# Turning the attention probabilities by a product with a diagonal matrix of inverse sums, in a two-layer hybrid backbone

## The chip, the cores and the metric

One core of a Trainium2 chip runs the whole kernel. The metric is the device time of one execution in microseconds (us), less is better. The core's engines go by short names: PE multiplies matrices (PEld is its loading of the stationary operand), DVE is the vector engine, ACT the scalar engine that also does the exponentials, POOL the general engine, and SP issues most of the transfers.

## What is computed

A backbone of two layers works on 512 latent tokens and 256 context tokens of width 1024, all in 32-bit floats. Each layer has a modulated RMSNorm, one input projection whose columns feed three head groups, an output projection with a gated residual, and a SwiGLU. The three groups are a latent attention (MLA, 4 heads; a latent token reads all 768 tokens, a context token the 256 of the context), a two-dimensional neighbourhood attention (NA, 4 heads; a block of 128 queries reads 256 local keys and the 256 context keys), and a gated delta rule in two directions. In the second layer context tokens aren't needed behind the attentions, so that only the 512 latent tokens are queries there. Both attentions end in the same way:

```python
def softmax_attention(q, k, v, scale):
    s = jnp.einsum('bqhd,bkhd->bhqk', q, k).astype(jnp.float32) * scale
    p = jax.nn.softmax(s, axis=-1).astype(v.dtype)
    return jnp.einsum('bhqk,bkhd->bqhd', p, v)
```

## The kernel before

Everything is unrolled; a tile framework orders the instructions of each engine in one list at build time, with a simulated timeline, and sets the semaphores. Large products are made of three products of reduced 32-bit parts (helper `mm3`; high and low halves), smaller ones of one product of plain 32-bit operands (helper `mm`, line 104, the line under which all products appear in the trace). A layer goes through these stages: input projection (tiles `acc_in`) with convolutions and the preparation of the delta rule; the neighbourhood attention (function `attention`, from line 850); the latent attention (from line 1183); the output projection (`acc_o`, `acc_o2`); the SwiGLU (`acc_gu`, `acc_d`).

The neighbourhood attention loops over 2 pairs of heads and, in each, over blocks of 128 queries (4 of latent tokens, and in the first layer 2 of context tokens). The latent attention loops in the same way. At each block the function `beside` may put other work into the order: one or two steps of the delta rule (`scan` and `inverse`, with the products `ks`, `yp`, `sp`, `qs`, `oa` on the full array and `pp`, `yq` on parts of it), by the hand-written counts in `DNS`; in the first layer's neighbourhood attention also two columns of modulation weights per block (`acc_ada`). So both attentions share PE and DVE with the delta rule. The first layer's latent attention also has the first part of the output projection (`acc_o`) beside it.

For one block and one head of a pair (`j`) the steps are these; lines of the neighbourhood attention first, of the latent attention second:

1. PE makes the scores in PSUM (`s_na`; `s_mla`).
2. DVE finds the row maximum (lines 870 to 876; 1199 and 1202), ACT writes the exponentials to the tile `pr` in SBUF and their sums to a small tile (877 and 878; 1206).
3. DVE adds the sums and takes the inverse (882 and 883; 1210 and 1212).
4. DVE multiplies `pr` by the inverse, one number per row, in place (884; 1213). A tile has 512 columns in the neighbourhood attention, 768 in the latent one, and 256 for context queries in both.
5. PE turns each block of 128x128 of `pr` with `PE.transpose` against the identity into PSUM (`tp_na`, 889; `tp_mla`, 1217): 4, 6, or 2 blocks for context queries.
6. ACT or DVE copies the result to SBUF (`pt`, 891; 1218), and behind both heads PE multiplies it with the values (`o_na`; `o_mla`).

`pr` has two buffers; the PSUM tiles of step 5 and of the last products share three.

Of the kernel before, what the change touches and what calls it, by code (L numbers as in the profile page):

```python
# [9 lines left out]
F32 = mybir.dt.float32  # L10
F32R = mybir.dt.float32r
AF = mybir.ActivationFunctionType
ALU = mybir.AluOpType
# [4 lines left out]
P = 128  # L18
D = 1024
KD = D // P  # L20
TL, TC = 512, 256
T = TL + TC
# [80 lines left out]
def mm(nc, out, lhsT, rhs, start=True, stop=True):  # L103
    nc.tensor.matmul(out, lhsT, rhs, start=start, stop=stop)  # L104
# [258 lines left out]
def layer(tc, nc, a, l, es_x, xT, env, nx):  # L363
    e = env
    V, S, G, PE = nc.vector, nc.scalar, nc.gpsimd, nc.tensor
    tt, stt, pool, C, ident, wtiles, gemm, dump, dram = e.tt, e.stt, e.pool, e.C, e.ident, e.wtiles, e.gemm, e.dump, e.dram
# [11 lines left out]
    def eb(name):  # L378
        tag = EB_TAG.get(name, "e")
        return psE.tile([P, 512], F32, tag=tag, name=name, bufs=EB[tag])  # L380
# [142 lines left out]
    tp = eb("ab_tp")  # L523
# [30 lines left out]
    tp = eb("gc")  # L554
# [286 lines left out]
    sn = None  # L841
# [5 lines left out]
    def attention():  # L847
        for pair in range(2):
            gm = gms[pair]
            o_na = sn.tile([P, T], F32, tag="o_na", name="o_na", bufs=1)  # L850
            grid = lambda t: t[:, LAT].rearrange("p (r c) -> p r c", c=GW)
            qh, ql, kh, kl = nqh[:, pair], nql[:, pair], nkh[:, pair], nkl[:, pair]
            for qt in range(nT // P):
                is_ctx = qt >= 4
                tok = slice(qt * P, (qt + 1) * P)
                c0 = (0, 8, 24, 32, 0, 0)[qt]
                var = (0, 1, 1, 2, 0, 0)[qt]
                vb = ((0, 1), (6, 7), (7, 8), (2, 3), (), ())[qt] + (4, 5)
                lo_ = 256 if is_ctx else 0
                pts = []  # L860
                for j in range(2):
                    hs = slice(64 * j, 64 * j + 64)
                    cutk = lambda t: grid(t)[hs, :, c0:c0 + 32].rearrange("p r (b c) -> p b r c", b=2)
                    s_ = att_bank("s_na")
                    if not is_ctx:
                        mm3(nc, s_[:, 0:256], (qh[hs, tok], ql[hs, tok]), (cutk(kh), cutk(kl)))
                    mm3(nc, s_[:, 256:512], (qh[hs, tok], ql[hs, tok]), (kh[hs, CTX], kl[hs, CTX]))
                    st_ = sn.tile([P, 8], F32, tag="st", name="st", bufs=4)
                    pr = sn.tile([P, 512], F32, tag="pr", name="pr", bufs=2)
                    V.reduce_max(out=st_[:, 0:1], in_=s_[:, 256:512], axis=AX.X)  # L870
                    if is_ctx:
                        V.tensor_scalar(out=st_[:, 2:3], in0=st_[:, 0:1], scalar1=-1.0, scalar2=None, op0=ALU.mult)
                    else:
                        V.tensor_tensor_reduce(out=pr[:, 0:256], in0=s_[:, 0:256], in1=gm[:, j, var].rearrange("p b r c -> p (b r c)"),
                                               scale=1.0, scalar=NEG, op0=ALU.add, op1=ALU.max, accum_out=st_[:, 1:2])
                        V.tensor_scalar(out=st_[:, 2:3], in0=st_[:, 0:1], scalar1=st_[:, 1:2], scalar2=-1.0, op0=ALU.max, op1=ALU.mult)
                        S.activation(out=pr[:, 0:256], in_=pr[:, 0:256], func=AF.Exp, bias=st_[:, 2:3], accum_out=st_[:, 3:4])
                    S.activation(out=pr[:, 256:512], in_=s_[:, 256:512], func=AF.Exp, bias=st_[:, 2:3], accum_out=st_[:, 4:5])
                    if is_ctx:
                        V.reciprocal(out=st_[:, 5:6], in_=st_[:, 4:5])  # L880
                    else:
                        tt(out=st_[:, 6:7], in0=st_[:, 3:4], in1=st_[:, 4:5], op=ALU.add)
                        V.reciprocal(out=st_[:, 5:6], in_=st_[:, 6:7])
                    V.tensor_scalar(out=pr[:, lo_:512], in0=pr[:, lo_:512], scalar1=st_[:, 5:6], scalar2=None, op0=ALU.mult)
                    tp = att_bank("tp_na")
                    nb = 2 if is_ctx else 4
                    for b in range(nb):
                        o2 = lo_ + b * P
                        PE.transpose(tp[:, b * P:(b + 1) * P], pr[:, o2:o2 + P], ident)  # L889
                    pt = sn.tile([P, 512], F32, tag="pt", name="pt", bufs=3)  # L890
                    (S.copy if j == 0 else V.tensor_copy)(out=pt[:, 0:nb * P], in_=tp[:, 0:nb * P])
                    pts.append(pt)
                o_ = att_bank("o_na")
                for b in range(len(vb)):
                    for j in range(2):
                        hd = 2 * pair + j
                        mm(nc, o_[j * 64:j * 64 + 64, 0:P], nav[:, vb[b], hd * 64:hd * 64 + 64], pts[j][:, b * P:(b + 1) * P],
                           b == 0, b == len(vb) - 1)
                if is_ctx:
                    S.copy(out=o_na[:, tok], in_=o_[:, 0:P])  # L900
                else:
                    S.copy(out=grid(o_na)[:, :, 16 * qt:16 * qt + 16], in_=o_[:, 0:P].rearrange("p (r c) -> p r c", c=16))
                if qt == nT // P - 1:
                    nc.sync.dma_start(out=d_o[2 + pair][:, 0:nT], in_=o_na[:, 0:nT])
                    if l == 0 and e.dbg is not None and "na" in e.dbg:
                        nc.sync.dma_start(out=e.dbg["na"][:, pair], in_=o_na)
                yield True
# [214 lines left out]
    sa = pool(es_w, f"sb_mla{l}", side=B_)  # L1122
# [31 lines left out]
    for pair in range(2):  # L1154
# [27 lines left out]
        for qt in range(nT // P):  # L1182
            beside(ada, sa)
            is_ctx = qt >= 4
            kst = ((CTX, 4, 2),) if is_ctx else ((LAT, 0, 4), (CTX, 4, 2))
            kcols = slice(TL, T) if is_ctx else slice(0, T)
            tok = slice(qt * P, (qt + 1) * P)
            pts = []
            for j in range(2):
                kh, kl, qh, ql = qk[j]  # L1190
                s8 = sa.tile([P, 8], F32, tag="st", name="st", bufs=4)
                pr = sa.tile([P, T], F32, tag="pr", name="pr", bufs=2)
# [17 lines left out]
                    tt(out=s8[:, 5:6], in0=den, in1=s8[:, 4:5], op=ALU.add)  # L1210
                    den = s8[:, 5:6]
                V.reciprocal(out=s8[:, 6:7], in_=den)
                V.tensor_scalar(out=pr[:, kcols], in0=pr[:, kcols], scalar1=s8[:, 6:7], scalar2=None, op0=ALU.mult)
                for i, (st_, b0, nb) in enumerate(kst):
                    tp = att_bank("tp_mla")
                    for b in range(nb):
                        PE.transpose(tp[:, b * P:(b + 1) * P], pr[:, (b0 + b) * P:(b0 + b + 1) * P], ident)
                    (V.tensor_copy if (b0 == 0) == (j == 0) else S.copy)(out=pt[:, st_], in_=tp[:, 0:nb * P])
                pts.append(pt)
            o_ = att_bank("o_mla")  # L1220
            b0 = kst[0][1]
# [245 lines left out]
```

## Time and profile before

| | |
|---|---|
| Median of 3 runs | 2146.63 us (2128.88, 2146.63, 2149.4) |
| The profiled execution | 2147.42 us, its span 2145.6 us |
| Mean granted clock of PE | 0.961 of full speed |
| Busy: PE, DVE, POOL, ACT | 2008.8, 1176.9, 758.7, 714.1 us |

The profile is of one execution on the chip. Times count from the start of the span. A busy PE isn't PE at its peak, since products are pipelined and their ends are modelled. The granted clock is the share of full speed that PE's throttle gave; 0.50 is the lower of its two levels.

### The profile page before, as it was taken

What the parts mean: (1) busy time and instruction counts of PE and PEld (TensorE: products, weight loads), DVE (VectorE), ACT (ScalarE), POOL (GpSimd) and SP (SyncE); (2) the same over time, 40 slices, a digit from 0 to 9 for tenths busy, and PEclk for the clock granted to TensorE, in tenths of its full rate; (3) what the DMA queues carried; (4) which work ended last, traced back from release to release, by engine and by line L of the source; (5) the groups of instructions that cost most, each with busy time, mean ns of one, the idle gap of its engine ahead of it and who ended that gap; (6) DMA issues with size and microseconds to landing.
All of it is one profiled execution on the core that took longest, in us unless ns stands there. A gap on an engine that the chain in (4) does not pass through costs nothing. (4 is left out here: it accounts for less than half of the span.)

```text
span 2145.6 us, 32031 instructions
## 1 busy us (share of the span) xinstructions
PE 2008.8 (94%) x12770; PEld 1699.3 (79%) x12770; DVE 1176.9 (55%) x2045; ACT 714.1 (33%) x1385; POOL 758.7 (35%) x540
## 2 busy tenths in 40 slices
PE   6899998998998999999999998889899889999998
PEld 4788787887787888888888876777688678888887
DVE  4888814768656447347343458882559654222123
ACT  5333323335444121121122344324334443222233
POOL 3465233113323222232323445623202252444444
PEclk9999998999999999999999999999679999999999
DMA  7324253542322435244342512424222232332332
GB/s 278 80 79 147 80 157 100 176 155 77 102 71 79 130 118 164 92 130 158 107 128 70 155 34 71 151 73 134 74 67 87 67 105 67 93 95 94 102 96 91
DMA packets 119309, 232.56 MB, mean 108 GB/s; under 512 B 30516, under 2 KB 55988, under 8 KB 119032
## 3 DMA queue, kind: packets, MB, share of 16 engines
q1 hardware_dynamic: 119160, 230.51, 34.2%
q8 instruction: 101, 1.65, 0.3%
q14 instruction: 48, 0.39, 0.1%
HBM read 199.46 MB, written 31.01 MB: 107 GB/s over the span
## 5 line engine op out<-in xcount | busy, mean ns | idle before, releaser
L217 POOL TENSOR_TENSOR wl<-wr,wh 128x1024 fp32r<-128x1024 f32 (+2 forms) x188 | 440.4, 2343 | 829.3 <-ACT wh L216 810.8
L216 ACT CAST wh<-wr 128x1024 fp32r<-128x1024 f32 (+2 forms) x190 | 193.5, 1019 | 717.9 <-PE acc_gu L104 289.2
L104 PE MATMUL acc_gu<-fh,wh 128*128 128x512 f32 (+1 forms) x1024 | 358.8, 353 | 9.6 <-ACT fh L304 8.7
L104 PE MATMUL acc_gu<-fl,wh 128*128 128x512 f32 (+1 forms) x1024 | 360.7, 353 | 4.1 <-DVE fl L305 4.1
L104 PE MATMUL acc_gu<-fh,wl 128*128 128x512 f32 (+1 forms) x1024 | 359.9, 352 | 0.0
L104 PE MATMUL acc_in<-hh,wh 128*128 128x512 f32 (+1 forms) x640 | 229.0, 362 | 16.9 <-ACT xp L491 6.2
L104 PE MATMUL acc_in<-hl,wh 128*128 128x512 f32 (+1 forms) x640 | 228.6, 358 | 3.0 <-DVE hl L305 2.0
L104 PE MATMUL acc_in<-hh,wl 128*128 128x512 f32 (+1 forms) x640 | 225.3, 356 | 2.1 <-POOL wl L217 2.0
L104 PEld LDWEIGHTS acc_gu<-fh,wh 128*128 128x128 f32 x1024 | 194.0, 190 | 37.2 <-ACT fh L304 11.0
L1348 DVE TENSOR_TENSOR av<-acc_gu,av 128x768 f32<-128x768 f32 (+1 forms) x44 | 36.3, 825 | 337.7 <-PE acc_gu L104 329.7
L104 PEld LDWEIGHTS acc_gu<-fl,wh 128*128 128x128 f32 x1024 | 195.0, 190 | 30.5 <-DVE fl L305 4.3
L104 PEld LDWEIGHTS acc_gu<-fh,wl 128*128 128x128 f32 x1024 | 194.8, 190 | 26.2
L104 PEld LDWEIGHTS acc_in<-hh,wh 128*128 128x128 f32 x640 | 125.1, 196 | 43.3 <-issue 8.1
L104 PE MATMUL acc_d<-al,wh 128*128 128x512 f32 (+1 forms) x444 | 157.2, 354 | 0.0
L104 PE MATMUL acc_d<-ah,wh 128*128 128x512 f32 (+1 forms) x444 | 157.2, 354 | 0.0
L104 PE MATMUL acc_d<-ah,wl 128*128 128x512 f32 (+1 forms) x444 | 156.1, 354 | 0.0
L254 DVE CUSTOM_DVE_ANT_0 junk<-wada,scb 128x1024 f32<-128x1024 f32 x112 | 144.1, 1286 | 7.9 <-DMA wada<-w_adaT 5.2
L104 PEld LDWEIGHTS acc_in<-hl,wh 128*128 128x128 f32 x640 | 125.7, 196 | 24.8 <-DVE hl L305 4.6
L104 PEld LDWEIGHTS acc_in<-hh,wl 128*128 128x128 f32 x640 | 124.8, 196 | 21.1 <-POOL wl L217 3.4
L1366 DVE SCALAR_TENSOR_TENSOR xT<-acc_d,mod,xT 128x512 f32<-128x512 f32 (+1 forms) x76 | 46.5, 634 | 155.4 <-PE acc_d L104 155.4
L501 DVE SCALAR_TENSOR_TENSOR cy<-xp,cw,cy 128x770 f32<-128x770 f32 (+1 forms) x96 | 118.9, 1239 | 22.5 <-ACT cy L499 20.4
L1352 DVE TENSOR_TENSOR al<-av,ah 128x768 fp32r<-128x768 f32 (+1 forms) x44 | 100.4, 2282 | 35.1 <-ACT ah L1351 35.1
(390 smaller groups left out, 3906.2 us busy)
## 6 DMA issues: line engine op xcount, KB each, us to landing
wr<-w_gu SPq DMA_DIRECT2D x88, 512.0 KB, 3.5
wada<-w_adaT SPq DMA_DIRECT2D x56, 512.0 KB, 3.3
wr<-w_in SPq DMA_DIRECT2D x48, 512.0 KB, 3.5
wr<-w_dn SPq DMA_DIRECT2D x32, 448.0 KB, 3.3
wada<-w_ada SPq DMA_DIRECT2D x24, 512.0 KB, 3.4
wada<-w_ada SPq DMA_DIRECT2D x8, 1024.0 KB, 8.3
wr<-w_dn SPq DMA_DIRECT2D x16, 512.0 KB, 3.5
xT<-xT SPq DMA_DIRECT2D x16, 384.0 KB, 5.3
```

The source lines that it names most:

```text
L104: nc.tensor.matmul(out, lhsT, rhs, start=start, stop=stop)
L216: S.copy(out=hi[:, sl], in_=raw[:, sl])
L217: eng.tensor_tensor(out=lo[:, sl], in0=raw[:, sl], in1=hi[:, sl].bitcast(F32), op=ALU.subtract)
L254: V.tensor_tensor_reduce(out=junk, in0=w, in1=scb[:, s], scale=1.0, scalar=0.0, op0=ALU.mult, op1=ALU.add, accum_out=mod[l][:, part, j, s: ...
L501: stt(out=y[:, :wid], in0=xp[:, j:j + wid], scalar=w_(j), in1=y[:, :wid], op0=ALU.mult, op1=ALU.add)
L1348: tt(out=av[:, :nT], in0=accs[1][:, :nT], in1=av[:, :nT], op=ALU.mult)
L1352: after.append(tt(out=l_[:, :nT], in0=av[:, :nT], in1=h_[:, :nT].bitcast(F32), op=ALU.subtract))
L1366: stt(out=xT[:, m, st_], in0=acc, scalar=mod[l][:, 5, m, s:s + 1], in1=xT[:, m, st_], op0=ALU.mult, op1=ALU.add)
```

## The change

Step 4 is taken away. Instead DVE multiplies the identity, a constant tile of 128x128, by the inverse of each row into a new tile `dg` (two buffers), a diagonal matrix. Step 5 becomes a product of each block of `pr` with `dg`: `mm(out, lhsT, rhs)` gives the transpose of `lhsT` times `rhs`, which is the turned block with each column multiplied by the inverse of its query. Copies and later products stay as they are.

```diff
@@ attention()
-                    V.tensor_scalar(out=pr[:, lo_:512], in0=pr[:, lo_:512], scalar1=st_[:, 5:6], scalar2=None, op0=ALU.mult)
+
+                    dg = sn.tile([P, P], F32, tag="dg", name="dg", bufs=2)
+                    V.tensor_scalar(out=dg, in0=ident, scalar1=st_[:, 5:6], scalar2=None, op0=ALU.mult)
                     tp = att_bank("tp_na")
                     nb = 2 if is_ctx else 4
                     for b in range(nb):
                         o2 = lo_ + b * P
-                        PE.transpose(tp[:, b * P:(b + 1) * P], pr[:, o2:o2 + P], ident)
+                        mm(nc, tp[:, b * P:(b + 1) * P], pr[:, o2:o2 + P], dg)
@@ latent attention
-            kcols = slice(TL, T) if is_ctx else slice(0, T)
...
                 V.reciprocal(out=s8[:, 6:7], in_=den)
-                V.tensor_scalar(out=pr[:, kcols], in0=pr[:, kcols], scalar1=s8[:, 6:7], scalar2=None, op0=ALU.mult)
+                dg = sa.tile([P, P], F32, tag="dg", name="dg", bufs=2)
+                V.tensor_scalar(out=dg, in0=ident, scalar1=s8[:, 6:7], scalar2=None, op0=ALU.mult)
                 for i, (st_, b0, nb) in enumerate(kst):
                     tp = att_bank("tp_mla")
                     for b in range(nb):
-                        PE.transpose(tp[:, b * P:(b + 1) * P], pr[:, (b0 + b) * P:(b0 + b + 1) * P], ident)
+                        mm(nc, tp[:, b * P:(b + 1) * P], pr[:, (b0 + b) * P:(b0 + b + 1) * P], dg)
```

## Rows read from the trace of the kernel before

**Rows 1.** The page, part 1: busy us, share of the span, instructions.
```profile
PE 2008.8 (94%) x12770; PEld 1699.3 (79%) x12770; DVE 1176.9 (55%) x2045; ACT 714.1 (33%) x1385; POOL 758.7 (35%) x540
```
**Rows 2.** Windows: stretch, its length, busy us by engine, PEclk, DMA share, GB/s.
```profile
362.00:482.00 120.00, 119.20 (x1483) 100.13 (x1482) 80.17 (x259) 40.71 (x137) 18.39 (x24) 1.00 0.51 162
515.00:560.00 45.00, 41.68 (x294) 32.19 (x293) 32.04 (x84) 22.72 (x77) 7.49 (x13) 0.91 0.31 103
580.00:642.00 62.00, 62.00 (x430) 52.92 (x429) 34.30 (x89) 24.95 (x59) 17.11 (x9) 1.00 0.20 62
1507.00:1520.00 13.00, 4.48 (x41) 3.55 (x39) 10.92 (x15) 5.84 (x14) 12.05 (x8) 0.86 0.55 184
...
1527.00:1578.00 51.00, 51.00 (x336) 43.34 (x336) 21.98 (x66) 13.18 (x44) 3.12 (x3) 0.50 0.13 42
```
**Rows 3.** Chain that ended last, second layer's latent attention: start us, us, step.
```profile
1635.57 0.53 DVE pr L1213
...
1640.94 0.66 PE tp_mla L1217 x6
...
1698.88 0.85 PE tp_mla L1217 x6
...
1701.41 1.29 DVE pr L1213
```
**Rows 4.** Groups by form, DVE: the scaling. Busy us, mean ns | idle before.
```profile
L1213 DVE TENSOR_SCALAR pr<-pr,st 128x768 f32<-128x768 f32 x32 | 21.9, 684 | 0.8
...
L884 DVE TENSOR_SCALAR pr<-pr,st 128x512 f32<-128x512 f32 x32 | 20.6, 647 | 0.8
...
L1213 DVE TENSOR_SCALAR pr<-pr,st 128x256 f32<-128x256 f32 x8 | 2.8, 362 | 0.1
L884 DVE TENSOR_SCALAR pr<-pr,st 128x256 f32<-128x256 f32 x8 | 2.7, 347 | 0.1
```
**Rows 5.** Line 1142: its group by form; then all it did (ns min/median/max).
```profile
L1142 DVE TENSOR_SCALAR wup<-wup,sml 128x128 f32<-128x128 f32 x16 | 5.6, 391 | 0.5 <-DMA wup<-w_qup 0.4
...
L1142 DVE TENSOR_SCALAR wup<-wup,sml x18: 269/284/2035, 486.0 to 1630.8; 128x128 f32<-128x128 f32 x16, 128x512 f32<-128x512 f32 x2
```
**Rows 6.** The tile pr: PE's transposes, ns min/median/max, first and last start.
```profile
L1217 PE MATMUL tp_mla<-cst,pr x208: 270/273/477, 517.0 to 1719.5; 128*128 128x128 f32 x104
...
L889 PE MATMUL tp_na<-cst,pr x144: 271/273/477, 363.5 to 1600.3; 128*128 128x128 f32 x144
```
**Rows 7.** Groups by form, PE: a product of the delta scan.
```profile
L104 PE MATMUL sp<-w,kt 128*128 128x128 f32 x160 | 26.7, 316 | 2.1 <-DVE w L1035 2.0
```
**Rows 8.** Timeline at the full clock: start us, us from first to last end.
```profile
1598.14 1.06 PE L104 MATMUL sp<-w,kt 128*128 128x128 f32 x8
...
1599.93 0.60 PE L889 MATMUL tp_na<-cst,pr 128*128 128x128 f32 x4
```
**Rows 9.** Timeline at the lower clock, PE.
```profile
1531.58 1.11 PE L889 MATMUL tp_na<-cst,pr 128*128 128x128 f32 x4
```
**Rows 10.** Windows of the tile tp_na alone: PE, PEld, DVE, ACT, then PEclk.
```profile
362.00:482.00 120.00, 11.13 (x80) 9.47 (x80) 7.20 (x12) 6.17 (x12) 1.00 0.51 162
...
1520.00:1578.00 58.00, 7.54 (x28) 5.14 (x28) 2.76 (x4) 1.76 (x3) 0.53 0.13 42
1578.00:1606.00 28.00, 3.88 (x24) 2.57 (x24) 2.06 (x3) 1.76 (x3) 1.00 0.17 55
```
**Rows 11.** Windows of the tile tp_mla alone.
```profile
580.00:642.00 62.00, 8.12 (x56) 6.33 (x56) 5.28 (x10) 4.58 (x10) 1.00 0.20 62
```
**Rows 12.** Timeline, DVE, beside a busy POOL.
```profile
1515.18 2.30 DVE L882 TENSOR_TENSOR st<-st 128x1 f32<-128x1 f32 x1
```
**Rows 13.** Timeline, PE, ahead of the clock's rise at 1578.
```profile
1573.24 2.08 PE L104 MATMUL ks<-S,dn_k 128*128 128x128 f32 x8
```
**Rows 14.** Timeline, PE, ahead of the clock's rise near 1687.
```profile
1685.28 1.49 PE L1217 MATMUL tp_mla<-cst,pr 128*128 128x128 f32 x6
```
**Rows 15.** Windows, as in rows 2.
```profile
1680.00:1688.00 8.00, 5.92 (x21) 4.61 (x19) 5.72 (x12) 2.80 (x9) 3.95 (x6) 0.57 0.01 3
```

## The prediction, made before the result was known

> **What bounds the kernel now.** I read the page's busy shares first: PE is busy 94% of the span [rows 1]. PE's bar is modelled and proves little by itself, so I went to the stretches in which the two attentions run and looked at PE, DVE and the granted clock in each [rows 2]. In the first layer's neighbourhood attention (362 to 482 us) PE is busy 119.2 of 120 us and DVE 80. In the first layer's latent attention PE has idle time from 515 to 560 (41.7 of 45), and none from 580 to 642, where the output projection runs beside it (62.0 of 62). In the second layer's neighbourhood attention PE is nearly idle from 1507 to 1520, while DVE works 10.9 and POOL 12.0 of 13 us; from 1527 to 1578 PE is busy throughout, but at a granted clock of 0.50, the lower of its two levels (1.2 GHz, not 2.4). In the second layer's latent attention neither engine is full, and the chain of waits has to tell which one leads [rows 3]: between 1635 and 1702 it goes seven times through a row of six transposes and six times through the DVE instruction that the change replaces. So the change takes work from DVE, which leads in a few short stretches, and gives work to PE, which leads in most.
>
> **What the change removes.** 80 DVE instructions that multiply a tile of probabilities by the inverse: 32 of 512 columns and 8 of 256 at line 884, 32 of 768 and 8 of 256 at line 1213, together 20.6 + 2.7 + 21.9 + 2.8 = 48.0 us [rows 4]. In their place come 80 of 128x128 from SBUF to SBUF. The same form exists at line 1142: 0.39 us on the mean, 0.28 in the middle of its times (two wider ones among them) [rows 5]. On means, 48.0 - 80 x 0.39 = 16.8 us of DVE time go. The waits stay the same in number: the new instruction waits for the same inverse, and PE waits for it as it waited for the scaled tile. Nothing new stands ahead of anybody on DVE's queue; the diagonal has two buffers and comes free when PE has used it, as the tile of probabilities does now. The link between inverse and PE gets shorter, by 0.26 us per tile in the neighbourhood attention and 0.29 in the latent one.
>
> **What it adds.** 144 transposes at line 889 and 208 at line 1217 [rows 6] become products of f32 operands. The trace shows what such a product is: sp of the delta scan is called 80 times in this shape (20 chunks that go on, 4 heads) and appears as 160 instructions [rows 7]. A product is two instructions, a transpose one. Their pitch: 8 of sp take 1.06 us, 4 transposes 0.60; with 0.27 for one alone, (1.06 - 0.27) / 7 = 0.11 and (0.60 - 0.27) / 3 = 0.11 [rows 8]. A block costs 0.112 us more on PE at the full clock, and at the lower one (1.11 - 0.48) / 3 = 0.21 more [rows 9]. For all 352 blocks that is 39.4 us at the full clock.
>
> A page of the Trainium skill speaks against this step: "Perfetto Trace Analysis", section Transposes, asks that a transpose be made as one and not as a standard matmul, since a transpose skips the arithmetic. The trace agrees, with twice the instructions at the same pitch.
>
> **Where the added time shows.** Block counts by stretch are in the trace [rows 10, 11].
> 1. First layer, neighbourhood: 80 blocks with PE full: 80 x 0.112 = +9.0. DVE has 40 us of idle time there, so that its relief buys nothing.
> 2. First layer, latent, beside the output projection: 56 blocks, PE full: +6.3.
> 3. First layer, latent, 515 to 560: the other 56 blocks, 6.3 us of PE; half of that layer's 24 DVE instructions, 8 of 768 and 4 of 256, give 8 x 0.68 + 4 x 0.36 - 12 x 0.39 = 2.2 back. Neither engine is full; I take half of each: +3.1 - 1.1 = +2.0 (bounds -2.2 and +6.3).
> 4. Second layer, neighbourhood: 28 blocks at the lower clock: 28 x 0.21 = +6.0. 24 after it, at the full one: +2.7. The other 12 fall before 1520, where PE waits: 0 (at most +1.3). DVE's instructions are long there beside POOL, but a one-column one takes 2.3 us too [rows 12]: their length isn't the columns', and I expect no gain. Sum +8.7.
> 5. Second layer, latent: the seven rows of six transposes on the chain, 42 blocks: +4.7. The six DVE instructions on it, five near 0.6 us and one of 1.29, become 0.28: -5 x 0.3 - 1.0 = -2.5. Sum +2.2. The other 54 blocks lie behind DVE and ACT; without that cover they would add 6.0.
> Together 9.0 + 6.3 + 2.0 + 8.7 + 2.2 = +28.2.
>
> **The clock.** 51 us of the second layer's neighbourhood attention run at the lower level. At the full one they would take 51 x 0.112 / 0.213 = 27 us, 24 less. That is the upper bound, zero the lower. The three timed runs lie at 2128.9, 2146.6 and 2149.4; the lowest is 17.7 under the median, which would fit a run in which this spell was shorter. What PE did just before the clock rose at 1578 was 16 full-array product instructions in a row, ks (8 in 2.08 us) and qs [rows 13]; in the spell these are mixed with products on parts of the array. The change puts twice as many full-array instructions into each tile's turn, so that the clock may rise earlier in some executions. I count a third of the 24: -8. I don't take all, because a transpose is full-array work too, and the other rise in an attention came right behind transposes: six of tp_mla at 1685.3 [rows 14], in a stretch of 8 us with a mean clock of 0.57 that ends at the full level [rows 15].
>
> The page "TensorE: Matmul & The Clock Gate" of the Trainium skill, Part 4: PE-mode transpose, says that a transpose doesn't count as PE-busy as a matmul does. By that page the change gives the clock work that it didn't see before; what would follow is the first rival. The rise named last speaks against it.
>
> **The sum.** The profiled execution took 2147.4 us (span 2145.6, 1.8 around it), 0.8 over the median of the runs. 2147.4 + 28.2 - 8 = 2167.6; less 0.8 for the median: 2167. That is 0.9% slower. A measurement of this kernel can tell about 1% (21.5 us) from no change, so the forecast lies at the edge of what can be told.
>
> **Rivals.**
> - *The lower clock goes away in the attentions* (the other sign). Place: 1527 to 1578, and two short spells in the latent attentions, near 546 and near 1684, of some 6.9 us each (0.86 of 8, as the mean of 0.57 has it). Price: 28.2, less 28 x 0.10 = 2.8 since no block pays the lower level's pitch, less 24, less half of 13.8: -5.5, so 2142, on the median 2141: faster, not slower. It decides once some 56 us of lower clock vanish (25.4 / 0.45), which is nearly all. For it: PE would do more full-array products in each spell. Against it: the transposes ahead of the rise near 1687, and that the clock falls after PE was idle (1507 to 1520), which products don't cure.
> - *DVE leads in all of the latent attention.* The six DVE steps on the chain speak for it, PE's 62.0 of 62 from 580 to 642 against it. Then the 40 instructions of line 1213 give 24.7 - 40 x 0.39 = 9.1 back and PE's blocks there cost nothing: 9.0 + 8.7 - 9.1 = +8.6, without help from the clock: 2155 on the median.
> - *All that PE gets shows.* 352 blocks, 28 of them at the lower clock: 39.4 + 2.8 = +42.2, nothing given back: 2189. For it: PE is busy in nearly every stretch, and a tile's blocks end 0.4 us later (4 x 0.11) before its copy can start. Against it: PE's idle time from 515 to 560 and the DVE steps on the chain.
> - That a product costs no more than a transpose, so that only DVE's relief is left (a third of 16.8 on the path: 2141), contradicts the 160 instructions for 80 calls.
>
> **Chances.** Forecast 0.54 (its own range 2156 to 2180), lower clock gone 0.13, DVE leading 0.15, all of PE's work 0.15, product as cheap as a transpose 0.03. The range from 2141 to 2187 leaves out about half of the first and of the third rival and of the last, some 0.17. Slower by over 1% (above 2168): a little under half of the forecast, and the third rival: 0.42. Faster by over 1% (under 2125) needs the lower clock gone and DVE's relief on the path as well: 0.06. Within 1%: 0.52.
>
> **What would show it.** Lines 884 and 1213 of before gone, 80 instructions for dg near 0.28 us (longer beside POOL); 288 instructions for tp_na and 416 for tp_mla at the pitch of sp; DVE's busy sum some 17 us lower. The first layer's neighbourhood attention takes 9 us longer with PE still full, the part beside the output projection 6 longer. The clock still falls near 1516 and rises sooner after it. Wrong would be: the first of these stretches not longer (then PE isn't what bounds it); a granted clock near 1.00 throughout the second layer's attentions (then the first rival); or the spell as long as before (then 2175).

## The result, and the profile after

The change takes 2164.74 us (median of 9 runs, 2157.26 to 2171.45), the kernel before 2147.81 (9 runs beside them). The ratio is 1.0088, with a 95% interval of 1.0061 to 1.0115: 0.9% slower, 18.9 us by that ratio (2147.81 x 0.0088; the medians lie 16.9 apart, and differences of medians and differences by a ratio are named as such below). The forecast's sum was +20.2 (28.2 - 8). The profiled execution, 2171.45 us, is the slowest of the nine; its span is 2169.7, 24.1 more than that of before.

What the instructions did is what the forecast said. Page, part 1, of the kernel after (it answers to [rows 1]):

```profile
PE 2038.7 (94%) x13122; PEld 1738.6 (80%) x13122; DVE 1166.0 (54%) x2045; ACT 717.1 (33%) x1385; POOL 757.0 (35%) x540
```

PE has 352 instructions more, one per block, and 29.9 us more busy time; DVE is busy 10.9 us less. The groups by form of the kernel after, where busy us and mean ns stand ahead of the second bar (they answer to [rows 4] and [rows 6]):

```profile
L104 PE MATMUL tp_mla<-dg,pr 128*128 128x128 f32 x416 | 56.7, 283 | 2.2 <-DVE dg L1215 1.1 <-ACT fs L1084 1.0
...
L104 PE MATMUL tp_na<-dg,pr 128*128 128x128 f32 x288 | 42.4, 300 | 3.4 <-DVE dg L886 3.4
...
L1215 DVE TENSOR_SCALAR dg<-cst,st 128x128 f32<-128x128 f32 x40 | 15.8, 394 | 0.9
...
L886 DVE TENSOR_SCALAR dg<-cst,st 128x128 f32<-128x128 f32 x40 | 14.8, 371 | 0.6
```

The 80 diagonals take 15.8 + 14.8 = 30.6 us (forecast 31.2), and the products come two to a block.

Where the time went is read from the four stretches with the attentions. Windows from the first `tp_na` of a layer to the first `acc_mv` (neighbourhood attention), and from there to the first `acc_gu` (latent attention and output projection). Columns: stretch, length, busy us of PE, PEld, DVE, ACT, POOL, granted clock, DMA share, GB/s. First the kernel before:

```profile
364.00:489.00 125.00, 120.63 (x1496) 101.53 (x1495) 83.94 (x263) 42.30 (x139) 21.76 (x26) 1.00 0.52 168
489.00:666.00 177.00, 161.05 (x1047) 133.08 (x1047) 118.67 (x260) 83.52 (x223) 59.28 (x50) 0.95 0.23 71
1507.00:1613.00 106.00, 96.22 (x888) 82.66 (x887) 63.46 (x152) 33.11 (x96) 22.70 (x18) 0.73 0.22 71
1613.00:1763.00 150.00, 136.12 (x922) 112.58 (x921) 102.00 (x219) 67.29 (x187) 48.74 (x48) 0.98 0.27 85
```

The same four of the kernel after:

```profile
362.00:497.00 135.00, 131.96 (x1570) 113.39 (x1570) 80.47 (x260) 42.30 (x139) 20.90 (x25) 0.97 0.48 153
497.00:693.00 196.00, 178.93 (x1166) 152.66 (x1166) 117.46 (x260) 85.05 (x223) 59.19 (x51) 0.93 0.20 63
1534.00:1629.00 95.00, 87.83 (x963) 77.97 (x961) 59.12 (x153) 32.64 (x95) 22.63 (x18) 0.90 0.28 85
1629.00:1792.00 163.00, 148.81 (x1008) 128.04 (x1008) 101.08 (x219) 72.29 (x195) 49.16 (x49) 0.95 0.25 77
```

Three of the four are longer, by 10, 19 and 13 us, and the second layer's neighbourhood attention is 11 us *shorter*, although it got 64 of the blocks. Its granted clock tells why: 0.73 before, 0.90 after. A mean of 0.73 over 106 us is 57 us at 0.50 (106 x 0.27 / 0.5), a mean of 0.90 over 95 is 19. These 57 us are two spells, a short one and a long one (51.2 us), and "the spell" of a kernel below is all the lower clock of this stretch. So one stretch gained from the clock about what another lost, and the sum hides both.

The table collects these stretches for the profiled execution of each kernel tried, with the exact borders; in brackets the us at the lower clock within. The fifth column runs from the second layer's first `acc_mv` to the end (brackets: up to `acc_gu` only), since a few us move over that inner border. The last column goes by all runs of a kernel and is explained below.

| Kernel | NA, layer 1 | latent + projection, layer 1 | NA, layer 2 | from there to the end | at equal clock, to before |
|---|---|---|---|---|---|
| before | 125.3 (0) | 176.9 (16.2) | 106.1 (58.0) | 532.6 (6.8) | 0 |
| before, second profile | 124.4 (0) | 177.0 (18.3) | 106.1 (58.0) | 532.6 (6.8) | -2 (one run) |
| after | 135.5 (6.8) | 195.9 (27.9) | 95.0 (18.5) | 540.3 (15.6) | +33 |
| after, second profile | 132.4 (3.2) | 192.2 (14.7) | 89.7 (13.7) | 538.9 (6.8) | +31 (one run) |
| NA half alone | 135.3 (9.2) | 174.6 (4.5) | 90.9 (13.7) | 526.6 (0) | +11 |
| latent half alone | 124.3 (0) | 182.2 (6.9) | 85.9 (20.5) | 544.9 (13.7) | +16 |
| PE part alone | 134.9 (0) | 193.0 (17.5) | 103.8 (34.1) | 538.1 (6.8) | +40 |
| DVE part alone | 129.6 (10.3) | 175.3 (18.1) | 85.2 (17.1) | 524.9 (0) | -6 |
| before + idle products | 125.5 (0) | 175.9 (11.9) | 85.0 (6.8) | 532.3 (13.7) | +1 |
| after + idle products | 139.7 (20.5) | 191.4 (10.5) | 90.8 (0) | 534.9 (0.3) | +37 |
| PE part + idle products | 146.9 (30.7) | 190.9 (10.8) | 96.2 (0) | 539.8 (13.7) | +46 |
| after, reduced operands | 130.0 (7.5) | 171.4 (16.4) | 115.0 (81.9) | 540.1 (23.9) | 0 |
| after, reduced operands + idle products | 135.2 (19.1) | 170.4 (15.0) | 82.4 (3.4) | 538.6 (23.9) | +2 |
| before + idle products, latent half reduced | 125.2 (0) | 176.5 (20.5) | 83.6 (3.4) | 539.3 (17.1) | +11 |

In stretches that PE bounds, 1 us at the lower clock costs 0.47 us, since work at a pitch of 0.213 would run at 0.112 [rows 8, 9].

Each run has a mean granted clock of its own, and 2 x (1 - clock) x its time are its us at 0.50. Over 62 runs of the kernel before, the time goes up by 0.45 us with each such us, so that the price holds about as well for the kernel as a whole. The last column takes 0.47 us for each us at 0.50 off every run and gives the mean as a difference to the kernel before, whose 62 runs then lie at 2067 with a spread of 2 us. It is an estimate, good to some 3 us, of what a change costs when the clock is left out.

### The profile page after: what moved, and what is told of

It is laid out like the page before. It is cut to its first block, busy times and chain, and to the rows that moved or that the text cites. A ratio compares the mean times of both kernels' runs of the same rounds, so it can differ in the third digit from the quotient of the medians.

```text
span 2169.7 us, 32726 instructions
## 1 busy us (share of the span) xinstructions
PE 2038.7 (94%) x13122; PEld 1738.6 (80%) x13122; DVE 1166.0 (54%) x2045; ACT 717.1 (33%) x1385; POOL 757.0 (35%) x540
## 5 line engine op out<-in xcount | busy, mean ns | idle before, releaser
L104 PEld LDWEIGHTS acc_in<-hh,wh 128*128 128x128 f32 x640 | 124.6, 196 | 44.3 <-ACT xp L491 7.9
L104 PEld LDWEIGHTS acc_in<-hl,wh 128*128 128x128 f32 x640 | 125.3, 196 | 24.7 <-DVE hl L305 4.6
L501 DVE SCALAR_TENSOR_TENSOR cy<-xp,cw,cy 128x770 f32<-128x770 f32 (+1 forms) x96 | 118.4, 1234 | 20.6 <-ACT cy L499 18.5
```

The costliest lines, as they stand in the source:

```text
L501: stt(out=y[:, :wid], in0=xp[:, j:j + wid], scalar=w_(j), in1=y[:, :wid], op0=ALU.mult, op1=ALU.add)
```

## The experiments

Two theories stood against each other. Theory 1: nearly all that PE gets shows, DVE's relief gives little, and a long spell at the lower clock in the second layer's neighbourhood attention, which happens to shorten, pays a part of it back. Theory 2: DVE's relief is large and pays PE's work back. Theory 3 came after the first four runs: the long spell costs some 20 us, and any kernel that gets past it is that much faster, whatever it turns the blocks with. A further question was whether the spell goes because a transpose is replaced by a product.

### Each half alone

Neighbourhood attention alone (the first hunk of the diff), then latent attention alone (the second).

> The change in the neighbourhood attention alone, the latent attention as before. Theory 1 (PE's added work sets the time, the clock of the second layer gives a part back): first layer's neighbourhood attention 9 us longer, the second layer's -11 to +9, so a ratio to the kernel before of 1.000 to 1.008; the latent stretches as long as before. Theory 2 (DVE's relief pays PE's work back): 0.997 to 1.001. If the order of the work around it matters more than either, the first layer's latent attention gets longer too though nothing was changed in it.

> The change in the latent attention alone. Theory 1: 1.005 to 1.010, nearly all of it in the first layer, where the trace of the changed kernel shows 19 us more from the start of the latent attention to that of the SwiGLU; the second layer's neighbourhood attention as before, with its long spell at the lower clock. Theory 2: 0.996 to 1.001. With the run of the neighbourhood attention alone the differences to the kernel before should add up to the whole change's 17 us within some 6 us, else the two parts act on each other.

The first took 2132.72 us (ratio 0.9931, 0.9909 to 0.9953), *faster* than before; the second 2145.56 (1.0007, 0.9984 to 1.003). By their ratios the halves sum to -14.8 + 1.5 = -13.3 us, the whole to +18.9: they don't add. The first lies outside both theories' ranges; the second lies in that of theory 2, and the spell that it should have kept is short. The windows say why. Second layer's neighbourhood attention with the latent half alone, which changes no line of this stretch's code:

```profile
1514.00:1600.00 86.00, 77.27 (x891) 67.37 (x888) 62.28 (x151) 33.33 (x96) 21.97 (x18) 0.88 0.29 88
```

It takes 86 us for 106, at 0.88 for 0.73. Either half alone shortens the long spell, and that can be gained once only. Outside this stretch the profiles of the halves are 3.5 and 19.1 us longer than that of before, 22.6 together, and the two pairs of profiles of the whole 35.2 and 23.5. At equal clock the halves cost 11 + 16 = 27 us, the whole 33.

The code of the stretch is the same, but not the order of its work: the framework orders the whole program anew for each kernel, and PE's order here is another in every edited kernel (before and its second profile have the same). The first run of `pp` behind the first `yp`, kernel before, then latent half alone:

```profile
1523.41 0.90 PE L104 MATMUL pp<-mix,LP 32*32 32x32 f32 x26
```

```profile
1530.27 2.39 PE L104 MATMUL pp<-mix,LP 32*32 32x32 f32 x50
```

### PE's part and DVE's part alone

PE's part: the division on DVE stays, and each block becomes a product with the identity.

```diff
-                        PE.transpose(tp[:, b * P:(b + 1) * P], pr[:, o2:o2 + P], ident)
+                        mm(nc, tp[:, b * P:(b + 1) * P], pr[:, o2:o2 + P], ident)
```

The latent attention has the same edit. DVE's part: the 128x128 instruction in place of the wide one, with transposes against its result. A second operation makes the identity of it again, so the probabilities aren't divided.

```diff
-                    V.tensor_scalar(out=pr[:, lo_:512], in0=pr[:, lo_:512], scalar1=st_[:, 5:6], scalar2=None, op0=ALU.mult)
+                    V.tensor_scalar(out=dg, in0=ident, scalar1=st_[:, 5:6], scalar2=0.0, op0=ALU.mult, op1=ALU.is_gt)
...
-                        PE.transpose(tp[:, b * P:(b + 1) * P], pr[:, o2:o2 + P], ident)
+                        PE.transpose(tp[:, b * P:(b + 1) * P], pr[:, o2:o2 + P], dg)
```

> PE's part alone: DVE divides the probabilities as before, and each block is then multiplied with the identity by a product in place of the transpose. Theory 1: some 30 us over the kernel before (1.012 to 1.019), that is, the 352 more instructions of 0.112 us with four fifths of them showing, and 5 to 15 us more than the whole change. Theory 2 (DVE's relief is large): 40 us or more over before (1.019 up). The rule that transposes don't count for the clock has the second layer's neighbourhood attention at the full clock for most of its length here; if they count, a spell of 15 to 50 us at the lower clock stays.

> DVE's part alone: the scaling of the probabilities is replaced by the same small DVE instruction as in the change, which here writes the identity again from the inverse (one where it is over zero), and PE turns the blocks with transposes against it. The division of the probabilities by their sums is left out. Theory 1: 0 to 8 us faster than before (0.996 to 1.000). Theory 2: 15 us or more faster (0.993 or less). The rule that transposes don't count for the clock has the long spell of the second layer as before (some 51 us at the lower clock); if what counts is how the work lies, it may differ.

PE's part took 2186.81 us (1.0182, 1.0151 to 1.0214), in theory 1's range: +39.1 by its ratio and +40 at equal clock, against 39.4 for all 352 blocks at the full clock and 28.2 for the forecast's sum, DVE's relief taken off. Its spell is 34.1 us, in the range named for the case that transposes do count for the clock; where the order of the work also changes, that doesn't show which rule holds. DVE's part took 2126.31 (0.9897, 0.9873 to 0.992): -22.1, in theory 2's range and outside theory 1's, but more than the 16.8 us of DVE time that go away altogether. So it can't be DVE's time alone; at equal clock 6 us of it are left, and the windows name the rest. DVE's part, the two neighbourhood attentions:

```profile
366.00:496.00 130.00, 125.89 (x1493) 104.75 (x1492) 80.47 (x260) 42.19 (x139) 20.27 (x25) 0.96 0.50 160
...
1515.00:1601.00 86.00, 78.93 (x894) 67.32 (x893) 60.47 (x153) 33.04 (x96) 22.57 (x18) 0.90 0.30 90
```

In the first layer the relief buys nothing (130 for 125 us, with 10 us at the lower clock that before didn't have: less 0.47 x 10.3 it is 124.8). In the second 20.9 us go, with the spell down from 58.0 to 17.1, and every block of this stretch is still a transpose.

PE's part, first layer:

```profile
365.00:500.00 135.00, 131.42 (x1579) 112.21 (x1579) 87.44 (x263) 41.95 (x139) 21.59 (x26) 1.00 0.50 155
500.00:693.00 193.00, 175.84 (x1159) 148.65 (x1159) 118.83 (x258) 84.32 (x222) 58.60 (x50) 0.95 0.20 63
```

At the full clock the neighbourhood attention grows by 134.9 - 125.3 = 9.6 us, for 80 blocks that the forecast put at 9.0. The latent attention and the projection grow by 16.1 at the same granted clock, where the forecast had 8.3 and all 112 blocks make 112 x 0.112 = 12.5. Nothing of PE's work is hidden there. What the 3.6 beyond the blocks are stays open. In the second layer's latent attention half of it is hidden: +5.5 to the end (532.6 to 538.1), where its 96 blocks make 10.8.

### Second profiles of both kernels

> The kernel before once more, for a second profile. Theory 3: the runs of this kernel near 2147 have the long spell (40 us or more at the lower clock in the second layer's neighbourhood attention), those near 2128 to 2136 a short one of some 20 us. Rival: the spell is as long in a fast run as in the others, and what varies lies elsewhere.

> The changed kernel once more, for a second profile. If the 28 us at the lower clock in the first layer's latent attention belong to the order of its work, they are there again (20 to 35 us); if they are chance of one execution, they fall to the 5 to 18 us of the kernels with one half of the change or none, and the kernel takes 2158 to 2163.

One run each, 2150.05 and 2157.14 us. The long spell in the kernel before isn't a chance of one execution: 106.1 us with 58.0 at the lower clock, twice. The question put to this run, whether the quicker executions of before have a short spell, stays open, since this one wasn't among them. They have less of the lower clock: 12 of the 62 runs lie at 2126 to 2138 us, with a mean clock of 0.963 to 0.970, where those above 2145 and up to 2151 have 0.958 to 0.961. So the same order of work, too, can run with up to some 40 us less at 0.50; in which stretch is not shown. After, the short spell comes again as well. Second layer's neighbourhood attention, second profile of after:

```profile
1527.00:1616.00 89.00, 83.61 (x956) 74.51 (x955) 56.65 (x153) 32.80 (x95) 21.89 (x18) 0.92 0.30 88
```

What differs between the two executions of the kernel after is the lower clock, mostly elsewhere: 14.7 us of it for 27.9 in the first layer's latent attention. By these two executions those 28 us don't belong to the order of its work.

### Filling PE's wait

What does PE do as the clock falls? The kernel before, timeline of PE (start, us, what, in square brackets the idle time ahead and what ended it):

```profile
1515.40 0.63 PE L889 MATMUL tp_na<-cst,pr 128*128 128x128 f32 x4 [2.21 <-DVE pr L884]
1520.09 1.12 PE L889 MATMUL tp_na<-cst,pr 128*128 128x128 f32 x4 [4.07 <-DVE pr L884]
```

It waits 2.2 and 4.1 us for the probabilities, and 4 transposes take 0.63 us before and 1.12 after. Windows of the kernel before at the two falls of the clock, columns as above:

```profile
1516.50:1523.30 6.80, 3.21 (x14) 2.82 (x14) 6.61 (x11) 0.15 (x1) 3.60 (x3) 0.50 0.14 51
1523.30:1526.70 3.40, 2.23 (x48) 1.84 (x46) 3.23 (x11) 0.71 (x3) 0.00 (x0) 1.00 0.26 77
1526.70:1577.90 51.20, 51.20 (x342) 43.58 (x338) 21.89 (x66) 13.48 (x45) 3.12 (x3) 0.50 0.13 42
```

The clock falls in the second wait, comes back for 3.4 us and falls again for the long spell. So I gave PE work for these waits: products of the full array whose result nobody uses, 10 and 18 for the two heads of one block, written to the bank that the transposes then overwrite. A small product ahead of them (`d0`) reads the sums of the exponentials, so that they begin when these are there.

```diff
+                    if l == 1 and pair == 0 and qt == 1:
+                        d0 = PE.matmul(tp[:, 0:2], kT[:, 0, 0:P], st_[:, 3:5], start=True, stop=True)
+                        with tc.issue_after(d0.ins):
+                            for _ in range((10, 18)[j]):
+                                mm(nc, tp[:, 0:P], kT[:, 0, 0:P], kT[:, 0, 0:P])
```

> The kernel before, with 28 idle products (10 and 18, of full size, results overwritten) put on PE in the second layer's neighbourhood attention, in the two waits for DVE between 1512 and 1520 us, in which PE stood idle just before its clock fell. The order of the other work stays. Theory 3 (the long spell at the lower clock is kept up by the mix of work behind that idle time and costs some 20 us; any kernel that gets past it is that much faster, whatever it turns the blocks with): the clock does not fall there, the stretch of 106 us takes 80 to 88, and the kernel some 18 us less than before (0.989 to 0.994). Rival: the clock falls there whether PE has work in those two waits or not, because the work behind them is thin; then the time is that of before or up to 4 us more (1.000 to 1.002).

The kernel before with these idle products takes 2126.81 us: 0.9923 (0.9887 to 0.9958), the fastest version here that computes everything. Its timeline of PE, and its window of the stretch:

```profile
1512.47 4.44 PE L104 MATMUL tp_na<-dn_k 128*128 128x128 f32 x20
...
1517.79 4.26 PE L104 MATMUL tp_na<-dn_k 128*128 128x128 f32 x36
1521.89 0.60 PE L894 MATMUL tp_na<-cst,pr 128*128 128x128 f32 x4
```

```profile
1507.00:1592.00 85.00, 81.82 (x950) 71.93 (x948) 61.44 (x152) 33.28 (x96) 22.10 (x18) 0.96 0.28 89
```

The first 20 instructions have a pitch of 0.22 (4.44 / 20), the lower level; the next 36 one of 0.12; the transposes behind them take 0.60. So the clock still falls once, for 6.8 us and earlier, and the long spell doesn't come. The stretch is 85 us for 106, and the whole is 16.5 us faster by its ratio (20.4 between the medians); at equal clock it is level with before. That is about the long spell's price, and it went without one change at a transpose.

What takes the spell away is not settled by this. The five kernels with idle products have 0 to 6.8 us at the lower clock in this stretch, the nine profiles without them 13.7 to 81.9. But the order of the other work did not stay, as the expectation has it: twelve products of the scores stand ahead of the first of the two waits in the kernel before, and all but one of them behind the second here. With the latent half alone PE's two waits are unfilled, 1.5 and 3.6 us, and the spell is 20.5 us for 58.0. The same 28 products in another place, or the order held, were not tried.

Then the same addition in the kernel after, and in PE's part alone, so that all stand without the long spell:

> The changed kernel with the same 28 idle products in the same place. Theory 3: with the spell out of both, the change costs what PE's second instructions cost, less what DVE's relief buys in the latent attentions: 30 to 38 us over the kernel before with idle products (2126.8), so 2157 to 2165 (1.004 to 1.009 of before), the second layer's neighbourhood attention at 90 to 94 us. Rival (the idle products are worth the same 20 us to any kernel): 2140 to 2147.

> PE's part alone, with the idle products: the kernel before with idle products (2126.8) in which each block is multiplied with the identity by a product in place of the transpose, behind the division on DVE. If PE's 352 more instructions show in full, +36 to +42, so 2163 to 2169 (1.007 to 1.010 of before), and DVE's relief is then what lies between this and the changed kernel with idle products (2158.8): 4 to 10 us. If DVE's relief is large, as the runs without idle products have it (21 us for DVE's part alone), 2172 or more; if it is nothing, 2156 to 2161.

After with idle products: 2158.84 us (1.0078 to before, 1.0048 to 1.0108). PE's part with them: 2179.77 (1.015, 1.012 to 1.018). Against before with idle products the change costs 2158.84 - 2126.81 = 32.0 us between the medians, which is what theory 3 said (30 to 38); PE's part costs 53.0, and the step from PE's part to the change gives 20.9 back (by the ratios 48.7 and 15.5). Taken as it stands, that would be the large relief of DVE. But the 53.0 are more than 39.4; in its profile 30.7 us of the first layer's neighbourhood attention are at the lower clock, of which before has none (14 us at 0.47). In the four stretches of the attentions PE's part has 55.2 us at the lower clock, the change 31.3 and before with idle products 32.4: the 32.0 are a comparison at nearly the same clock, the other two aren't. At equal clock the step from PE's part to the change is 46 - 37 = 9 us, and 40 - 33 = 7 without idle products; with the 6 of DVE's part alone, DVE's relief is 6 to 9 us. The first window of PE's part with idle products:

```profile
364.00:511.00 147.00, 144.67 (x1581) 123.93 (x1579) 87.35 (x262) 41.99 (x139) 21.57 (x25) 0.90 0.45 141
```

The idle products take away one spell; they don't make the clock equal in all stretches, so that plain differences of these kernels are good to some 10 us, not to one. The kernels without the spell bear out the order of the theory (all of PE's work shows, DVE's relief gives part of it back), not its last digit.

### A product of one instruction

To take the second instruction out, `pr` and `dg` got the reduced 32-bit type (the probabilities are rounded to it), with a tile of its own for the biased scores.

```diff
-                    pr = sn.tile([P, 512], F32, tag="pr", name="pr", bufs=2)
+                    pr = sn.tile([P, 512], F32R, tag="pr", name="pr", bufs=2)
+                    sg = sn.tile([P, 256], F32, tag="sg", name="sg", bufs=1)
...
-                    dg = sn.tile([P, P], F32, tag="dg", name="dg", bufs=2)
+                    dg = sn.tile([P, P], F32R, tag="dg", name="dg", bufs=2)
```

> The whole change with reduced 32-bit operands: the probabilities and the diagonal are written in the reduced form, so that a product is one instruction, and the neighbourhood attention's biased scores get a tile of their own. The turned probabilities are rounded to the reduced form (a part of the computation is changed by that). Theory 1 (what the change costs is PE's second instruction per block): the pitch is that of a transpose or less, PE's count is as before, and the time is that of DVE's part alone, 2115 to 2130 (0.985 to 0.992). Rival (the new order costs, not PE's instructions): 2140 or more.

A block is now one instruction. Timeline of PE at the full clock, then the window of the stretch:

```profile
1515.14 1.01 PE L104 MATMUL tp_na<-dg,pr 128*128 128x128 f32 x8
```

```profile
1515.00:1630.00 115.00, 109.27 (x902) 95.88 (x901) 57.53 (x154) 33.89 (x97) 22.83 (x18) 0.64 0.23 69
```

Less 0.275 for one alone, 8 of them have a pitch of (1.01 - 0.275) / 7 = 0.105, that of a transpose. In the first layer's latent attention 5.5 us go (176.9 to 171.4, at the same us of lower clock): there DVE's relief shows once PE pays nothing for it. Yet the kernel takes 2175.1 us (1.0128, 1.0081 to 1.0176), slower than the change and in the rival's range, since the spell grew to 81.9 us. At equal clock it is level with the kernel before, 33 us under the change: so the 33 go with PE's second instructions, and the 6 us of DVE's relief don't show.

With the idle products, first the whole of it, then the latent half alone on the kernel before:

> The change with reduced operands, with the same 28 idle products. Theory 3: its time of 2175 is the work at the lower clock (82 us in the second layer's neighbourhood attention, 24 in the latent one); if the idle products take away the first, that stretch falls from 115 to 80 to 86 us and the kernel to 2138 to 2146. Rival: the spell comes back behind them, since a product of reduced operands puts half as much full-array work on PE as one of plain operands; then 2165 to 2180.

> The kernel before with the 28 idle products, and the change with reduced operands in the latent attention alone. If a product of reduced operands costs what a transpose costs and DVE's relief is worth some 8 us in the latent attentions, 2115 to 2122 (0.985 to 0.988), under the kernel before with idle products. Rival: the clock stays low for longer in the latent attentions, as in the run with reduced operands in both: 2130 or more.

They took 2141.89 us (0.9991, 0.9963 to 1.0019), as theory 3 said, and 2139.77 (0.9988, 0.996 to 1.0016), in the rival's range. The first is 33 us under the same kernel without idle products, but both are 13 to 15 over the kernel before with the idle products alone. The first of them has the lower clock in other stretches: 19.1 us in the first layer's neighbourhood attention, where that kernel has none, and 23.9 for 13.7 in the second layer's latent attention; at equal clock the two are level. The second is not explained by the clock: it stays 11 us over at equal clock. Of these, 9 lie between the start of the first layer's SwiGLU and the second layer's neighbourhood attention (666 to 1517 us, 851 us for 842), which its edit doesn't touch and where both have 43 to 44 us at the lower clock. Why that part is longer stays open. The first of them, second layer:

```profile
1519.00:1601.00 82.00, 80.42 (x959) 72.41 (x959) 56.54 (x154) 33.04 (x96) 22.73 (x18) 0.98 0.29 92
1601.00:1758.00 157.00, 141.87 (x916) 119.47 (x914) 99.26 (x216) 67.93 (x187) 46.66 (x47) 0.92 0.26 80
```

The neighbourhood attention is the shortest of all, 82 us, and the next stretch at 0.92 (0.98 before) takes part of it back. In the kernels with a cheaper product the lower clock lies elsewhere; it didn't end.

## Why the prediction was right in its sum, and where its steps failed

**The sum.** 18.9 us measured, 20.2 forecast; 2164.74 lies in the likeliest case's own range. But two of its terms failed in opposite directions: the work cost some 33 us at equal clock, for 28.2 forecast, and the clock gave some 14 back, for 8. The agreement to 1 us is luck.

**What the change removes: right.** 80 diagonals of 30.6 us for 31.2; DVE's groups lose 48.0 - 30.6 = 17.4 us for 16.8. DVE's busy time on the page fell by 10.9 only, for the 17 named as a sign; it counts overlapping instructions once, and the durations of all DVE instructions in the trace sum to 1261.2 us before and 1243.4 after, 17.8 less.

**What it adds: right.** Twice the instructions, 352 more; PE's part alone cost 39.1 us, and 352 blocks at 0.112 make 39.4. By stretch it agrees less well (16.1 for 12.5, and 5.5 for 10.8, above).

**Term 1, first layer's neighbourhood attention: right.** +9.0 forecast; +9.6 with PE's part alone at the full clock, +10.2 and +8.0 in the two profiles of after, and nothing back from DVE.

**Terms 2 and 3, first layer's latent attention: too small.** +8.3 forecast, +19.0 and +15.2 measured in the two pairs of profiles. The step "Neither engine is full; I take half of each" failed. PE's part alone grew by 16.1 here, more than the bound of 12.5 for all blocks. In the first profile of after 11.7 us more at the lower clock add 0.47 x 11.7 = 5.5; with the clock priced out the two pairs have +13.5 and +16.9 and PE's part +15.5, so that the 2.2 us of DVE's relief that term 3 counts on don't show.

**Term 5, second layer's latent attention: too small.** +2.2 forecast; +7.7 and +6.3 from there to the end (8.8 us more at the lower clock make 4.1 of the first; the second pair has the same clock). "The other 54 blocks lie behind DVE and ACT; without that cover they would add 6.0" is the step that failed. The chain that ended last, of after, from 1630 to 1790 us:

```profile
by line: PE acc_o L104 26.2%; PE tp_mla L104 13.8%; PE s_mla L104 9.9%; PE o_mla L104 9.2%; issue 3.0%; PE oa L104 2.9%; PE acc_mq L104 2.5%; ACT pr L1207 2.4%; PE ks L104 2.4%; PE sp L104 2.2%; PE acc_mv L104 2.2%; PE qs L104 1.8%; DVE q L
...
1654.80 1.34 PE tp_mla L104 x12
...
1658.98 1.34 PE tp_mla L104 x12
...
1709.23 2.58 PE tp_mla L104 x12
```

Six blocks take 1.34 us where they took 0.66, and the product's share of the chain is 13.8%, some 22 of 160 us. The six DVE steps of [rows 3] are gone from it, and 15 of the 16 rows of six blocks lie on it, where the kernel before had seven. PE's part alone, with DVE as long as before, adds 5.5 for the 4.7 of the seven rows. So that reading was right for the kernel before, but what was behind DVE became the leader as soon as DVE was shorter and PE longer.

**Term 4 and the clock: the gain too small.** +8.7 - 8 forecast, -11.1 and -16.4 measured. The products' share of it was about right: without the long spell the stretch takes 90.8 us with the change and 85.0 without, +5.8, or +9 if the 6.8 us of lower clock in the latter are allowed for; the two pairs of profiles leave +7.5 and +4.4 with the clock priced out. The step that failed is "I count a third of the 24": 39.5 and 44.3 us less at the lower clock are 18.6 and 20.8 us. The clock falls as forecast, and rises much sooner. Windows of after, around the spell:

```profile
1534.00:1546.00 12.00, 6.77 (x63) 5.74 (x61) 9.45 (x21) 5.35 (x13) 10.62 (x7) 1.00 0.69 237
1546.00:1563.00 17.00, 15.77 (x114) 14.32 (x114) 6.41 (x20) 3.27 (x10) 2.20 (x3) 0.50 0.12 32
1563.00:1629.00 66.00, 65.29 (x788) 57.91 (x787) 43.27 (x113) 24.02 (x72) 9.81 (x9) 0.99 0.24 71
```

17 us at 0.50, where [rows 2] show a spell of 51. Part of it came back elsewhere: in all four stretches of the attentions the lower clock fell only from 81.0 to 68.8 us in the first pair of profiles (to 38.4 in the second profile of after). With the spell out of both kernels the change costs 32.0 us instead of 18.9, so that the clock gave some 13 us, for 8 forecast; all runs at equal clock say 33 and 14.

**The reason given for the clock: not borne out.** The forecast said that twice as many full-array instructions in a tile's turn let the clock rise sooner. The spell shortens as much where no product is added in its stretch (latent half: 20.5 us; DVE's part: 17.1), and less where the products are added and DVE is left as it was (PE's part: 34.1). It grows where the blocks are one-instruction products (81.9). The row that the reason was read from is weaker than it was taken: behind the 16 products of ks and qs, the last eight of which start at 1575.1 and end at 1577.0, PE makes products of the scores ahead of the rise near 1578. The rule of the Trainium skill that was weighed, "TensorE: Matmul & The Clock Gate", Part 4: PE-mode transpose, that a transpose doesn't count as PE-busy, isn't needed for this: with all transposes in place the spell was 58.0, 20.5, 17.1 or 6.8 us, as the work around them lay. No run here holds the order of the work and changes the transposes alone, so the rule isn't refuted either. What this case shows is that profiles with the same order of PE's work in this stretch have nearly the same spell (58.0 twice; 18.5, 13.7 and 13.7; 6.8 and 3.4), and that it was shortest with idle products ahead of it. Whether the filled wait or the order does that, and why a spell ends after 17 or only after 51 us, stays open.

**The rivals.** *Lower clock goes away*: it went in the one place for the greater part (58.0 to 18.5 and 13.7 us), not in the latent attentions. Its 0.45 us for each us of lower clock isn't worked out there; by the pitches it is 0.47, which makes 54 us for its 56. *DVE leads in all of the latent attention*: fell, since PE's blocks cost all that they could in the first layer and half of it in the second. *All that PE gets shows* came nearest as to the products: 39.1 with PE's part alone (40 at equal clock) for its 42.2. It missed what was given back: some 14 us by the clock and 6 to 9 by DVE's relief. *Product as cheap as a transpose*: fell for plain 32-bit operands.

## What to carry to other kernels

Before the halves of a change are judged one by one, look at the granted clock of the stretches that neither touches: here a spell worth some 20 us shrank with most edits, each half alone looked free or better, and together they cost 19. Where each run has its mean granted clock, put a price on the lower clock and compare the rest. Such spells can also move because an edit elsewhere changes the order of the work, so compare that order before a spell is put down to the edit. Work moved from an engine with idle time to the one that is full showed here in full in the sum (40 us for a count of 39.4), though not stretch by stretch; price it at its whole count first and argue each deduction. And where the fullest engine waits a few us for another and then runs on at half its clock, idle products in that wait are worth a trial: 28 of them came with 16.5 us, a ratio of 0.9923.

## What the runs showed of the hardware that was not expected

- The lower clock didn't go by the edited instructions here: a stretch with unchanged code, but with its work in another order, ran 58.0 us at 0.50 in the kernel before and 20.5 with an edit in another function.
- The time of an execution followed its granted clock: over 62 runs of the kernel before, 0.45 us for each us at 0.50.
- A product of reduced 32-bit operands, 128x128, has the pitch of a transpose (0.105 us); one of plain 32-bit operands takes two instructions, 0.22 in all. Cheaper products didn't make the kernel faster than the change, since the spell at the lower clock grew from 18.5 to 81.9 us; at equal clock they take its 33 us away.
- Small DVE instructions stretch: a diagonal takes 0.29 us in the middle of its times and up to 2.11. The times of the kernel after, min, median and max in ns:

```profile
L886 DVE TENSOR_SCALAR dg<-cst,st x40: 268/286/2110, 357.3 to 1613.6; 128x128 f32<-128x128 f32 x40
L1215 DVE TENSOR_SCALAR dg<-cst,st x40: 276/286/1756, 527.5 to 1752.3; 128x128 f32<-128x128 f32 x40
```
